# A hybrid decoder layer on one core: the output projection of the state-space heads two pairs at a time, v split for four heads at once, three pairs of split weight tiles

## The chip, the core and the metric

The kernel runs on one core of a Trainium2 chip. A core has a matmul engine (TensorE, PE in the profile, with its weight loads as PEld), VectorE (DVE), ScalarE (ACT), GpSimd (POOL) and SyncE (SP), which here only issues transfers. Each engine works through its own list of instructions in order; they wait for one another by semaphores. The metric is the device time of one execution in microseconds (us); lower is better.

## The reference

One decoder layer on 512 tokens of width 1024, in float32:

```python
h = rms_norm(x, norm_mix_w)
z, xbc, dt_raw, q, k, v, f_raw = jnp.split(h @ w_in, [...], axis=-1)
y_ssd = ssd_mixer(xbc, z, dt_raw, ...)      # 16 heads of 64, 2 groups, chunks of 128 tokens
y_fox = fox_mixer(q, k, v, f_raw, ...)      # 16 heads of 64, causal, with a forget gate
mixed = jnp.concatenate([y_ssd, y_fox], axis=-1)          # 512 x 2048
x = x + mixed @ w_out                                     # 2048 x 1024
hf = rms_norm(x, norm_ffn_w)
x = x + conv_gated_mlp(hf, w_up, ..., w_down)             # 1024 -> 2 x 2816 -> 1024
```

In the attention mixer, q and k are normalised per head, the cumulative sum of log forget gates is added to the logits (`cum[q] - cum[k]`), and `p @ v` follows a softmax. In the state-space mixer (SSD), each chunk of 128 tokens has a product within the chunk and one with the state that the chunks before it left; its output is gated by `silu(z)` and normalised per group.

## The kernel before

**Numbers in two parts.** Every matrix product is made of three matmuls of a reduced float32 type: a high part times a high part, high times low, low times high (`mm3`, lines L110, L111 and L112). Weights come from memory as tiles `wraw` of 128x1024 (512 KB, five buffers, a transfer on SP's queue, L101). `load_split` makes the high part `wh` on ACT (L104) and the low part `wl = wraw - wh` on DVE or POOL (L105); which of the two is a letter of the table `LOW_PART` ("d" is DVE, "p" POOL, and "p" where a key isn't in it), taken in turn. `wh` and `wl` have two buffers each in the pool `wp`; in the last stage, the down projection, `split_unit` adds a third of each from another pool (`pb`).

**Stages.** (1) To about 25 us: x comes in, is split in two, and the norm's scale is computed. (2) To about 225 us the SSD mixer in two groups of 8 heads. `ssd_proj` makes x, B and C (`feature_tile`, then a convolution over tokens on DVE, L351) and the gate (`token_block` into banks named pq, then `gz`, L374 to L376). `dt_f` makes the step sizes; its cumulative sum `cs` (L304, DVE) is read by a small matmul `pt` (L306). `ssd_scan` goes over four chunks; each ends with the normalised `y` (L441, DVE), a PE transpose `yT` (L446), and the parts `msh` and `msl` (L448, ACT, and L449, DVE), which the output projection multiplies. (3) To about 465 us the attention mixer, 16 heads. For each group of four heads `qk_proj` and `v_proj` project; `fox_qk` transposes a pair's k and q (`qkT`, L496), splits them, and copies the two parts of k to the other 64 partitions by two transfers (`ks`, L506); `fox_probs` makes the logits (`S`, L539 and L540) and the softmax; `fox_values` multiplies with v (`o`). A pair of heads gives 128 columns of `mixed`. Between heads, "fillers" with work that doesn't depend on that head are written. (4) The output projection `out_proj` is spread through (2) and (3): it takes one pair of 128-row slabs of `w_out`, and for each half of the 1024 columns and each of four blocks of 128 tokens it runs 6 matmuls of 512 columns into a bank `po` and adds it to `x2`, the residual (L254, DVE). SSD has pairs 0 to 3, attention 4 to 7. (5) The up projection with its convolution and gate, 494 to 743 us. (6) The down projection, in which half of the transfers of `w_down` tiles `T` are issued by POOL and add to what the tile holds (L809).

**PSUM.** `bank` gives one of three banks of 128x512 that the projections share (names g, pq, po, up, X); `mbank` one of four for the mixers' smaller products; `o` has one. 

**Order.** The program writes each engine's work in a certain sequence, but a scheduler then sets the order of the instructions, by a simulated timeline and by priorities (`urgent` puts scans and heads first). So an edit in one place moves instructions of every engine elsewhere. The number of names (as in `yT_990`) only tells one buffer's use from another's.

Of the kernel before, what the change touches and what calls it, by code (L numbers as in the profile page):

```python
# [9 lines left out]
F32R = mybir.dt.float32r  # L10
AF = mybir.ActivationFunctionType
ALU = mybir.AluOpType
# [3 lines left out]
P = 128  # L16
# [3 lines left out]
NTB = SEQ // P  # L20
# [8 lines left out]
HD = 64  # L29
# [5 lines left out]
ACT_SQ = (1, 3, 5, 7)  # L35
LOW_PART = {
    "feat": "pddddddddp",
    "o0": "dp",
    "o2": "dp",
    "o4": "pd",  # L40
    "o5": "pd",
    "o7": "pd",
    "qk1": "dppd",
    "qk2": "pppd",
# [11 lines left out]
def tile_hybrid_layer(  # L56
# [19 lines left out]
    nc = tc.nc  # L76
# [11 lines left out]
    def raw(ap):  # L88
        return ap.bitcast(F32)
# [9 lines left out]
    def load_split(src, sub=None):  # L99
        r = wp.tile([P, 1024], F32, tag="wraw", name="wraw", bufs=5)  # L100
        nc.sync.dma_start(r, src)  # L101
        h = wp.tile([P, 1024], F32R, tag="wh", name="wh")
        l = wp.tile([P, 1024], F32R, tag="wl", name="wl")
        act.copy(h, r)  # L104
        (sub or dve).tensor_tensor(out=l, in0=r, in1=raw(h), op=ALU.subtract)  # L105
        return h, l

    def mm3(o, ah, al, bh, bl, start, stop, grouped=True):
        kw = {} if grouped else {"skip_group_check": True}
        pe.matmul(o, ah, bh, start=start, stop=False, **kw)  # L110
        pe.matmul(o, ah, bl, start=False, stop=False, **kw)  # L111
        pe.matmul(o, al, bh, start=False, stop=stop, **kw)  # L112

    def bank(name="g"):
        return pg.tile([P, 512], F32, tag="g", name=name)
# [42 lines left out]

    px_ctx = ExitStack()
    px = px_ctx.enter_context(tc.tile_pool(name="px", bufs=1))  # L160
    first = [wp.tile([P, 1024], F32R, tag=t, name=t) for t in ("wh", "wl")]
    wdt = px.tile([P, NK, 64], F32R, tag="wdt", name="wdt")

    def load_x(k):
# [45 lines left out]
    for k in range(NK):  # L210
        pe.matmul(pdt[:64, :], wdt[:, k, :], xh[:, k, :], start=k == 0, stop=False, skip_group_check=True)
        pe.matmul(pdt[:32, :], wdt[:, k, 0:32], xl[:, k, :], start=False, stop=k == NK - 1, skip_group_check=True)
        c = slice(k * P, (k + 1) * P)
# [28 lines left out]
    def out_proj(pairs, m, halves=(0, 1)):  # L242
        for half in halves:
            ws = [load_split(wout[pair, half], sub=low_part("o%d" % pairs[0])) for pair in pairs]
            for tb in range(NTB):
                s = slice(tb * P, (tb + 1) * P)
                o = bank("po")
                for n, (h, l) in enumerate(ws):
                    for j in range(2):
                        k = 2 * n + j  # L250
                        c = slice(j * 512, (j + 1) * 512)
                        mm3(o, m[k][0][:, s], m[k][1][:, s], h[:, c], l[:, c], k == 0, k == 2 * len(pairs) - 1)
                dst = x2[:, tb, half * 512 : (half + 1) * 512]
                dve.tensor_add(dst, o, dst)  # L254

    pss_ctx = ExitStack()
    pss = pss_ctx.enter_context(tc.tile_pool(name="pss", bufs=1, reuse_waits="tile"))
# [212 lines left out]

    def v_proj(gi):
        tiles = token_block(wqkv[gi, 2], "v%d" % gi)
        v = [pa.tile([P, NTB, 2, 2 * HD], F32R, tag="v", name="v", bufs=4) for _ in range(2)]
        for pr in range(2):
            for tb in range(NTB):
                c = (tb % 2) * 256 + pr * P
                o = tiles[tb // 2][:, c : c + P].rearrange("p (h d) -> p h d", d=HD)
                act.activation(v[pr][:, tb, :, 0:HD], o, AF.Copy, scale=r[:, tb : tb + 1])
                dve.scalar_tensor_tensor(
                    out=v[pr][:, tb, :, HD:], in0=o, scalar=r[:, tb : tb + 1], in1=raw(v[pr][:, tb, :, 0:HD]),  # L480
                    op0=ALU.mult, op1=ALU.subtract,
                )
        return v

    LO, HI = slice(0, HD), slice(HD, P)
# [64 lines left out]
        return prob  # L550

    def fox_values(head, prob, v, osum):
        lh = head % 2
        own, other = HALVES[head % 2]
        where = {}
        for n, kbs in enumerate(((0,), (1, 3), (2,))):
# [45 lines left out]
    for tb in range(NTB):  # L602
        nc.sync.dma_start(x2[:, tb, :], x[tb * P : (tb + 1) * P, :])
    st1 = ssd_proj(1)
    for pair in range(2):
        out_proj((pair,), m0[2 * pair : 2 * pair + 2])
    with urgent():
        m1 = ssd_scan(1, *st1)
    qk, vs = {}, {}
# [22 lines left out]

    def end_head(n):
        with urgent():
            m = fox_values(n, probs.pop(n), vs[n // 4][n % 4 // 2], pairs[n // 2][2])
        if m is not None:
            mf.append(m)

    fillers = {0: ["q1"], 3: ["v1"], 4: ["q2", "v2"], 5: ["o0"], 8: ["q3"], 9: ["a", "o1"], 10: ["v3"], 12: ["o2"], 15: ["b"]}

    def fill(name):
        if name == "a":
            out_proj((2,), m1[0:2])
        elif name == "b":
            out_proj((3,), m1[2:4])
        elif name[0] == "q":
            project(int(name[1:]))
        elif name[0] == "v":
            project_v(int(name[1:]))
        else:  # L650
            g = int(name[1:])
            out_proj((4 + g,), mf[2 * g : 2 * g + 2])
# [62 lines left out]
        nc.sync.dma_start(rw[:, 0 : (UNITS[u][1] - UNITS[u][0]) * 512], part(q, u))  # L715
        return rw

    turn = [0]

    def split_unit(u, src):  # L720
        n = (UNITS[u][1] - UNITS[u][0]) * 512
        where = pb if turn[0] % 3 == 2 else wp
        turn[0] += 1
        h = where.tile([P, 1024], F32R, tag="wh", name="wh")
        l = where.tile([P, 1024], F32R, tag="wl", name="wl")
        act.copy(h[:, :n], src[:, :n])  # L726
        dve.tensor_tensor(out=l[:, :n], in0=src[:, :n], in1=raw(h[:, :n]), op=ALU.subtract)  # L727
        return h, l
# [225 lines left out]
```

## Time and profile before

| | |
|---|---|
| median of 3 runs | 847.28 us (845.74 to 851.2) |
| the profiled execution | 845.59 us |
| its span, first to last instruction | 843.8 us |
| mean granted TensorE clock | 0.998 |
| instructions | 12403, of these 4590 matmuls |

The profile is one execution, with the start and end of every instruction and what ended the idle time ahead of it. A row of a group has the line of the kernel, the engine, the operation, the tile it writes and those it reads, the shape and the count, then the group's busy time in us and the mean of one instruction in ns, and the idle time of the engine ahead of them with its releaser. The granted clock is the share of TensorE's full clock that the throttle let through.

### The profile page before, as it was taken

How to read it: one execution, taken by the hardware profiler on the slowest of the kernel's cores; microseconds unless marked ns; L12 is line 12 of the kernel's file. 1: busy time of each engine (PE TensorE's matmuls, PEld its weight loads, DVE VectorE, ACT ScalarE, POOL GpSimd, SP SyncE). 2: the span in 40 equal slices, each digit the busy share in tenths (PEclk: the TensorE clock that was granted, in tenths of full speed). 3: DMA queues.
4: the chain of work that ended last, by engine and by line, in shares of the span. 5: the costliest groups of instructions: out<-in, count | busy, mean ns of one | idle time of the engine just before them, and what ended most of it. 6: DMA issues, size and time to landing. Idle time of an engine off the chain costs nothing.

```text
span 843.8 us, 12403 instructions
## 1 busy us (share of the span) xinstructions
PE 810.0 (96%) x4590; PEld 696.6 (83%) x4590; DVE 630.9 (75%) x999; ACT 434.6 (52%) x830; POOL 291.4 (35%) x281
## 2 busy tenths in 40 slices
PE   6999989899989999999999999999999999998987
PEld 4888879779989898798898888888888888875766
DVE  7696998775779788997988767666666667875644
ACT  5456546443567675684575364444444444654432
POOL 3125253375445445135133413333333331332210
PEclk9999999999999999999999999999999999999999
DMA  8424322431442332333331222322222333599972
GB/s 313 164 76 130 100 101 76 133 105 50 140 123 86 104 101 92 96 112 107 95 101 51 95 81 100 99 99 89 91 97 100 100 100 109 160 304 240 241 169 88
DMA packets 32285, 101.63 MB, mean 120 GB/s; under 512 B 4129, under 2 KB 4961, under 8 KB 32225
## 3 DMA queue, kind: packets, MB, share of 16 engines
q1 hardware_dynamic: 28768, 89.31, 32.3%
q0 software_dynamic: 3456, 11.54, 7.0%
q8 instruction: 36, 0.59, 0.3%
q14 instruction: 25, 0.20, 0.1%
HBM read 94.44 MB, written 2.20 MB: 115 GB/s over the span
## 4 chain that ended last, share of the span: by engine, by line
PE 67%; DVE 13%; issue 7%; DMA 6%; POOL 3%; ACT 3%; SPq 0%; DVEq 0%; POOLq 0%; ACTq 0%
PE up L112 9%; PE up L110 9%; PE up L111 9%; DMA T<-in_wdown_dram 4%; PE pq L111 4%; PE pq L112 4%; PE pq L110 4%; PE po L112 3%; PE po L111 3%; PE po L110 3%; DVE xs L351 2%; PE o L580 1%; PE pT L566 1%; POOL ms L122 1%; PE Y L111 1%
## 5 line engine op out<-in xcount | busy, mean ns | idle before, releaser
L104 ACT CAST wh<-wraw 128x1024 fp32r<-128x1024 f32 x103 | 108.4, 1053 | 135.5 <-PE up L111 72.1
L110 PE MATMUL pq<-wh,xh 128*128 128x256 f32 x512 | 146.3, 288 | 0.0
L112 PE MATMUL pq<-wh,xl 128*128 128x256 f32 x512 | 146.2, 286 | 0.0
L111 PE MATMUL pq<-wl,xh 128*128 128x256 f32 x512 | 145.3, 284 | 0.6 <-DVE wl L105 0.6
L112 PE MATMUL up<-hh,wl 128*128 128x512 f32 (+1 forms) x368 | 140.2, 381 | 0.2 <-DVE wl L105 0.2
L111 PE MATMUL up<-hl,wh 128*128 128x512 f32 (+1 forms) x368 | 139.9, 380 | 0.0
L110 PE MATMUL up<-hh,wh 128*128 128x512 f32 (+1 forms) x368 | 139.8, 380 | 0.0
L105 POOL TENSOR_TENSOR wl<-wraw,wh 128x1024 fp32r<-128x1024 f32 x31 | 75.3, 2427 | 107.7 <-ACT wh L104 98.6
L105 DVE TENSOR_TENSOR wl<-wraw,wh 128x1024 fp32r<-128x1024 f32 x72 | 90.3, 1254 | 20.0 <-ACT wh L104 19.9
L111 PEld LDWEIGHTS pq<-wl,xh 128*128 128x128 f32 x512 | 97.8, 191 | 2.1 <-DVE wl L105 1.1
L110 PEld LDWEIGHTS pq<-wh,xh 128*128 128x128 f32 x512 | 97.5, 191 | 1.9 <-issue 1.2
L112 PEld LDWEIGHTS pq<-wh,xl 128*128 128x128 f32 x512 | 97.8, 191 | 0.7 <-issue 0.5
L112 PEld LDWEIGHTS up<-hh,wl 128*128 128x128 f32 x368 | 69.2, 188 | 13.8 <-DVE wl L105 0.4
L111 PEld LDWEIGHTS up<-hl,wh 128*128 128x128 f32 x368 | 69.2, 188 | 13.1
L110 PEld LDWEIGHTS up<-hh,wh 128*128 128x128 f32 x368 | 69.1, 188 | 13.1 <-issue 0.2
L765 DVE TENSOR_TENSOR up<-up,R 128x512 f32<-128x512 f32 x44 | 30.3, 691 | 57.0 <-PE up L112 57.0
L770 DVE SCALAR_TENSOR_TENSOR ua<-up,pc,ua 128x511 f32<-128x511 f32 (+1 forms) x88 | 67.1, 765 | 3.2 <-ACT ua L768 1.7
L526 POOL TENSOR_SCALAR bias<-cum,tokS 128x256 f32<-128x256 f32 (+1 forms) x32 | 22.4, 711 | 88.9 <-DVE nm L541 88.9
L254 DVE TENSOR_TENSOR x<-po,x 128x512 f32<-128x512 f32 x64 | 43.2, 683 | 10.1 <-PE po L112 9.5
L545 ACT ACTIVATE prob<-prob,nm 128x128 f32<-128x128 f32 (+1 forms) x64 | 35.9, 562 | 27.2 <-DVE nm L541 26.9
L780 POOL TENSOR_TENSOR ua<-ua 128x512 f32<-128x512 f32 x11 | 15.0, 1364 | 93.0 <-DVE ua L770 93.0
L727 DVE TENSOR_TENSOR wl<-T,wh 128x1024 fp32r<-128x1024 f32 (+1 forms) x24 | 26.9, 1134 | 26.2 <-ACT wh L726 26.2
(249 smaller groups left out, 1876.9 us busy)
## 6 DMA issues: line engine op xcount, KB each, us to landing
wraw<-in_wup_dram SPq DMA_DIRECT2D x44, 512.0 KB, 3.3
wraw<-in_wqkv_dram SPq DMA_DIRECT2D x24, 512.0 KB, 3.3
T<-in_wdown_dram POOLq DMA_DIRECT2D x20, 512.0 KB, 11.9
wraw<-in_wout_dram SPq DMA_DIRECT2D x16, 512.0 KB, 3.4
wraw<-in_wdown_dram SPq DMA_DIRECT2D x15, 512.0 KB, 4.6
wraw<-in_wxbc_dram SPq DMA_DIRECT2D x11, 512.0 KB, 4.0
T<-in_wdown_dram SPq DMA_DIRECT2D x10, 512.0 KB, 8.0
wraw<-in_wz_dram SPq DMA_DIRECT2D x8, 512.0 KB, 3.4
```

What stands on the lines that cost most here:

```text
L104: act.copy(h, r)
L105: (sub or dve).tensor_tensor(out=l, in0=r, in1=raw(h), op=ALU.subtract)
L110: pe.matmul(o, ah, bh, start=start, stop=False, **kw)
L111: pe.matmul(o, ah, bl, start=False, stop=False, **kw)
L112: pe.matmul(o, al, bh, start=False, stop=stop, **kw)
L254: dve.tensor_add(dst, o, dst)
L351: dve.scalar_tensor_tensor(out=dst[:, s:], in0=xp[:, : SEQ - s], scalar=half_w[:, cw + 3 - s : cw + 4 - s], in1=dst[:, s:], op0=ALU.mult, ...
L526: (dve if qb == 2 else pool).tensor_scalar(out=b, in0=cum[:, :n], scalar1=-1.0, scalar2=edge, op0=ALU.mult, op1=ALU.add)
L545: act.activation(p, p, AF.Exp, scale=-1.0, bias=nm[:, qb : qb + 1], accum_out=sm[:, qb : qb + 1])
L727: dve.tensor_tensor(out=l[:, :n], in0=src[:, :n], in1=raw(h[:, :n]), op=ALU.subtract)
L765: dve.tensor_mul(xp, o, R2)
L770: dve.scalar_tensor_tensor(out=a[:, s:], in0=xp[:, : SEQ - s], scalar=pc[:, cw + 2 - s : cw + 3 - s], in1=a[:, s:], op0=ALU.mult, op1=ALU.add,
```

## The change

1. `out_proj` for the SSD pairs takes two pairs in one accumulation: 12 matmuls go into a bank before it is added to `x2`. Blocks of tokens go in twos, so that two banks are open at once. Pairs 0 and 1 come together behind `ssd_proj(1)`, as before; pairs 2 and 3 come together, the left half of the columns as a filler at head 9 and the right half at head 15, where pair 2 and pair 3 stood. The attention pairs still go one at a time, with two blocks of tokens per step.
2. `v_proj` evacuates all four heads of a block of tokens by one ACT and one DVE instruction of 256 columns, where there were two of 128 on each.
3. `wh` and `wl` have three buffers in one pool throughout.
4. In `LOW_PART`, `o0` and `o2` go from "dp" to "d", and a key `o6` ("pd") is new.
5. The buffer for the descriptors of POOL's transfers is 1024 instead of 2048 bytes.

```diff
 LOW_PART = {
...
-    "o0": "dp",
-    "o2": "dp",
+    "o0": "d",
+    "o2": "d",
     "o4": "pd",
     "o5": "pd",
+    "o6": "pd",
     "o7": "pd",
...
-        h = wp.tile([P, 1024], F32R, tag="wh", name="wh")
-        l = wp.tile([P, 1024], F32R, tag="wl", name="wl")
+        h = wp.tile([P, 1024], F32R, tag="wh", name="wh", bufs=3)
+        l = wp.tile([P, 1024], F32R, tag="wl", name="wl", bufs=3)
...
     def out_proj(pairs, m, halves=(0, 1)):
         for half in halves:
             ws = [load_split(wout[pair, half], sub=low_part("o%d" % pairs[0])) for pair in pairs]
-            for tb in range(NTB):
-                s = slice(tb * P, (tb + 1) * P)
-                o = bank("po")
+            banks = {}
+            for t0 in (0, 2):
                 for n, (h, l) in enumerate(ws):
-                    for j in range(2):
-                        k = 2 * n + j
-                        c = slice(j * 512, (j + 1) * 512)
-                        mm3(o, m[k][0][:, s], m[k][1][:, s], h[:, c], l[:, c], k == 0, k == 2 * len(pairs) - 1)
-                dst = x2[:, tb, half * 512 : (half + 1) * 512]
-                dve.tensor_add(dst, o, dst)
+                    for tb in (t0, t0 + 1):
+                        s = slice(tb * P, (tb + 1) * P)
+                        if n == 0:
+                            banks[tb] = bank("po")
+                        for j in range(2):
+                            k = 2 * n + j
+                            c = slice(j * 512, (j + 1) * 512)
+                            mm3(
+                                banks[tb], m[k][0][:, s], m[k][1][:, s], h[:, c], l[:, c],
+                                k == 0, k == 2 * len(pairs) - 1,
+                            )
+                        if n == len(ws) - 1:
+                            dst = x2[:, tb, half * 512 : (half + 1) * 512]
+                            dve.tensor_add(dst, banks[tb], dst)
...
-        v = [pa.tile([P, NTB, 2, 2 * HD], F32R, tag="v", name="v", bufs=4) for _ in range(2)]
-        for pr in range(2):
-            for tb in range(NTB):
-                c = (tb % 2) * 256 + pr * P
-                o = tiles[tb // 2][:, c : c + P].rearrange("p (h d) -> p h d", d=HD)
-                act.activation(v[pr][:, tb, :, 0:HD], o, AF.Copy, scale=r[:, tb : tb + 1])
-                dve.scalar_tensor_tensor(
-                    out=v[pr][:, tb, :, HD:], in0=o, scalar=r[:, tb : tb + 1], in1=raw(v[pr][:, tb, :, 0:HD]),
-                    op0=ALU.mult, op1=ALU.subtract,
-                )
+        v = pa.tile([P, NTB, 4, 2 * HD], F32R, tag="v", name="v", bufs=2)
+        for tb in range(NTB):
+            c = (tb % 2) * 256
+            o = tiles[tb // 2][:, c : c + 256].rearrange("p (h d) -> p h d", d=HD)
+            act.activation(v[:, tb, :, 0:HD], o, AF.Copy, scale=r[:, tb : tb + 1])
+            dve.scalar_tensor_tensor(
+                out=v[:, tb, :, HD:], in0=o, scalar=r[:, tb : tb + 1], in1=raw(v[:, tb, :, 0:HD]),
+                op0=ALU.mult, op1=ALU.subtract,
+            )
...
-    for pair in range(2):
-        out_proj((pair,), m0[2 * pair : 2 * pair + 2])
+    out_proj((0, 1), m0)
...
-    fillers = {0: ["q1"], 3: ["v1"], 4: ["q2", "v2"], 5: ["o0"], 8: ["q3"], 9: ["a", "o1"], 10: ["v3"], 12: ["o2"], 15: ["b"]}
+    fillers = {
+        0: ["q1"], 3: ["v1"], 4: ["q2", "v2"], 5: ["o0"], 8: ["q3"], 9: ["a0", "o1"], 10: ["v3"], 12: ["o2"],
+        15: ["a1"],
+    }
...
-        if name == "a":
-            out_proj((2,), m1[0:2])
-        elif name == "b":
-            out_proj((3,), m1[2:4])
+        if name[0] == "a":
+            out_proj((2, 3), m1, halves=(int(name[1:]),))
...
-    turn = [0]
-
     def split_unit(u, src):
         n = (UNITS[u][1] - UNITS[u][0]) * 512
-        where = pb if turn[0] % 3 == 2 else wp
-        turn[0] += 1
-        h = where.tile([P, 1024], F32R, tag="wh", name="wh")
-        l = where.tile([P, 1024], F32R, tag="wl", name="wl")
+        h = wp.tile([P, 1024], F32R, tag="wh", name="wh", bufs=3)
+        l = wp.tile([P, 1024], F32R, tag="wl", name="wl", bufs=3)
...
-    nc = _bacc.Bacc("TRN2", target_bir_lowering=False, num_devices=1, dynamic_dma_scratch_size=2048)
+    nc = _bacc.Bacc("TRN2", target_bir_lowering=False, num_devices=1, dynamic_dma_scratch_size=1024)
```

The scheduler moves instructions with it. In the changed kernel the line numbers are a few higher (L101 becomes L102, L506 L513, L446 L454, the matmuls L111 to L113). Three places:

SP's queue where the first attention pair begins; `wraw` are the q, k and v weights, `cum` the forget gate's sums, `ks` the copies of k for the two heads of a pair. Before:

```order
L101 DMA wraw<-in_wqkv_dram 128x1024 x5
L512 DMA cum<-cf_d 128x512 x2
L101 DMA wraw<-in_wqkv_dram 128x1024
L512 DMA cum<-cf_d 128x512 x2
L101 DMA wraw<-in_wqkv_dram 128x1024
L506 DMA ks<-ks 64x1024 x2
L101 DMA wraw<-in_wqkv_dram 128x1024
```

and with the change:

```order
L102 DMA wraw<-in_wqkv_dram 128x1024 x5
L519 DMA cum<-cf_d 128x512 x2
L102 DMA wraw<-in_wqkv_dram 128x1024
L519 DMA cum<-cf_d 128x512 x2
L513 DMA ks<-ks 64x1024
L102 DMA wraw<-in_wqkv_dram 128x1024
L513 DMA ks<-ks 64x1024
```

The `wraw` that stood ahead of both `ks` now stands between them.

PE at the third transpose of the first scan (`yT_990`; `pq` is the gate's projection, `cb` the next chunk's product). Before:

```order
L110 MATMUL pq_1467<-wh_1471,xh_93 128x256
L111 MATMUL pq_1467<-wl_1472,xh_93 128x256
L112 MATMUL pq_1467<-wh_1471,xl_94 128x256
L446 MATMUL yT_990<-ident_75,y_969 128x128 x4
L411 MATMUL cb_1012<-cT_377,bT_376 128x128
```

and with the change:

```order
L111 MATMUL pq_1341<-wh_1399,xh_93 128x256
L112 MATMUL pq_1341<-wl_1400,xh_93 128x256
L113 MATMUL pq_1341<-wh_1399,xl_94 128x256
L454 MATMUL yT_990<-ident_75,y_969 128x128 x4
L419 MATMUL cb_1012<-cT_377,bT_376 128x128
```

The transpose now stands in the projection with weights `wh_1399`, the one ahead of that with `wh_1471`. Counted from the program's start, the matmuls of 256 and of 512 columns ahead of `pt` and of the first scan's transposes are:

| ahead of | before, 256 and 512 | with the change |
|---|---|---|
| `pt` | 97, 145 | 63, 145 |
| first `yT` | 192, 219 | 192, 187 |
| second | 194, 292 | 192, 266 |
| third | 303, 294 | 255, 294 |
| fourth (`yT_1039`) | 384, 307 | 370, 295 |

On DVE, ahead of `cs` there are three convolution steps fewer; ahead of the first `y` three convolution steps and two products `xp` fewer; of the second, three steps, one `xp` and one `xs` product; of the third, one `gz` and one `xs` product; of the fourth none.

PE at the first output projection. Before, where `po_1615` is the third block of tokens:

```order
L111 MATMUL po_1607<-wl_1596,msh_822 128x512
L112 MATMUL po_1607<-wh_1595,msl_823 128x512
L446 MATMUL yT_1039<-ident_75,y_1024 128x128 x4
L411 MATMUL cb_1768<-cT_1055,bT_1054 128x128
L110 MATMUL po_1615<-wh_1595,msh_822 128x512
L111 MATMUL po_1615<-wl_1596,msh_822 128x512
```

and with the change, where `po_1605` and `po_1612` are the first two blocks:

```order
L111 MATMUL pq_1468<-wh_1525,xh_93 128x256
L454 MATMUL yT_1039<-ident_75,y_1024 128x128 x4
L419 MATMUL cb_1752<-cT_1055,bT_1054 128x128
...
L112 MATMUL pq_1468<-wl_1526,xh_93 128x256
L113 MATMUL pq_1468<-wh_1525,xl_94 128x256
L111 MATMUL po_1605<-wh_1595,msh_822 128x512
L112 MATMUL po_1605<-wl_1596,msh_822 128x512
L113 MATMUL po_1605<-wh_1595,msl_823 128x512
```

The last transpose of the scan, which stood between two blocks of the output projection, now stands in the gate's projection ahead of it, and both weights' parts of the first two blocks come before the third block.

More of the change, by code (lines that the diff above doesn't have):

```diff
@@ L160, in tile_hybrid_layer @@
     px = px_ctx.enter_context(tc.tile_pool(name="px", bufs=1))
-    first = [wp.tile([P, 1024], F32R, tag=t, name=t) for t in ("wh", "wl")]
+    first = [wp.tile([P, 1024], F32R, tag=t, name=t, bufs=3) for t in ("wh", "wl")]
     wdt = px.tile([P, NK, 64], F32R, tag="wdt", name="wdt")
@@ L552, in fox_values @@
     def fox_values(head, prob, v, osum):
-        lh = head % 2
+        lh = head % 4
         own, other = HALVES[head % 2]
@@ L634, in end_head @@
         with urgent():
-            m = fox_values(n, probs.pop(n), vs[n // 4][n % 4 // 2], pairs[n // 2][2])
+            m = fox_values(n, probs.pop(n), vs[n // 4], pairs[n // 2][2])
         if m is not None:
             mf.append(m)
-    fillers = {0: ["q1"], 3: ["v1"], 4: ["q2", "v2"], 5: ["o0"], 8: ["q3"], 9: ["a", "o1"], 10: ["v3"], 12: ["o2"], 15: ["b"]}
+    fillers = {
+        0: ["q1"], 3: ["v1"], 4: ["q2", "v2"], 5: ["o0"], 8: ["q3"], 9: ["a0", "o1"], 10: ["v3"], 12: ["o2"],
+        15: ["a1"],
+    }
     def fill(name):
-        if name == "a":
-            out_proj((2,), m1[0:2])
-        elif name == "b":
-            out_proj((3,), m1[2:4])
+        if name[0] == "a":
+            out_proj((2, 3), m1, halves=(int(name[1:]),))
         elif name[0] == "q":
```

## The prediction

> **What bounds the kernel now.** I begin with the page's totals, since they say which engine a saving must reach.
>
> ```profile
> span 843.8 us, 12403 instructions
> PE 810.0 (96%) x4590; PEld 696.6 (83%) x4590; DVE 630.9 (75%) x999; ACT 434.6 (52%) x830; POOL 291.4 (35%) x281
> PE 67%; DVE 13%; issue 7%; DMA 6%; POOL 3%; ACT 3%; SPq 0%; DVEq 0%; POOLq 0%; ACTq 0%
> ```
>
> PE is busy 96% of the span, and the third line, the chain that ended last, runs on PE for 67%. The change keeps all 4590 matmuls, so it can gain no more than PE's gaps and its slow stretches. A table of stretches says where those are; its columns are start and end, length, the busy time (and instructions) of PE, weight loads, DVE, ACT and POOL, the granted clock, the DMA share and GB/s.
>
> ```profile
> 40.00:140.00 100.00, 95.03 (x595) 83.58 (x594) 89.08 (x126) 53.55 (x133) 39.62 (x26) 1.00 0.32 106
> 220.00:240.00 20.00, 17.06 (x130) 16.69 (x129) 12.24 (x26) 10.29 (x23) 11.59 (x14) 0.92 0.47 133
> 520.00:540.00 20.00, 20.00 (x90) 16.57 (x89) 13.67 (x18) 9.17 (x13) 6.42 (x6) 1.00 0.31 104
> ```
>
> In the up projection (520 to 540) PE has no gap: 90 matmuls of 512 columns in 20 us are 0.222 us each. I use 0.23 for a matmul of 512 columns. In the mixer there are gaps, and in 220 to 240 the granted clock falls to 0.92 as well. Over the first scan (40 to 140) DVE is nearly full: some 89 of 100 us. What PE waited for there, in us in total, times, and the longest:
>
> ```profile
> PE S L539 <- DMA ks<-ks: 3.4, 2, 2.9
> PE qkT L496 <- DVE tok L468: 2.5, 2, 1.3
> PE yT L446 <- DVE y L441: 1.7, 1, 1.7
> PE pt L306 <- DVE cs L304: 1.5, 1, 1.5
> PE po L110 <- ACT msh L448: 1.5, 1, 1.5
> PE po L110 <- DVE v L479: 1.2, 1, 1.2
> PE po L110 <- ACT th L375: 0.7, 1, 0.7
> PE pq L111 <- DVE wl L105: 0.6, 1, 0.6
> ```
>
> These eight rows, 13.1 us, are what the change can reach in the mixer.
>
> **The change part by part.** First the work on the engines beside PE.
>
> ```profile
> L254 DVE TENSOR_TENSOR x<-po,x 128x512 f32<-128x512 f32 x64 | 43.2, 683 | 10.1 <-PE po L112 9.5
> L105 POOL TENSOR_TENSOR wl<-wraw,wh 128x1024 fp32r<-128x1024 f32 x31 | 75.3, 2427 | 107.7 <-ACT wh L104 98.6
> L105 DVE TENSOR_TENSOR wl<-wraw,wh 128x1024 fp32r<-128x1024 f32 x72 | 90.3, 1254 | 20.0 <-ACT wh L104 19.9
> L478 ACT ACTIVATE v<-pq,r 128x128 fp32r<-128x128 f32 x32 | 11.4, 364 | 19.8 <-DVE v L479 13.1 <-PE pq L112 6.5
> L479 DVE SCALAR_TENSOR_TENSOR v<-pq,r,v 128x128 fp32r<-128x128 f32 x32 | 10.9, 347 | 4.2 <-ACT v L478 3.8
> L460 ACT ACTIVATE tok<-pq,r 128x256 f32<-128x256 f32 x32 | 15.1, 471 | 8.3 <-PE pq L112 8.3
> ```
>
> Adding two pairs in one accumulation removes 16 of the 64 adds: 16 x 0.683 = 10.9 us of DVE. Seven low parts go from POOL to DVE: 7 x 2.427 = 17.0 us off POOL, 7 x 1.254 = 8.8 us onto DVE. The wide v instructions are not in the trace. On ACT one of 256 columns stands in the tok row, 0.471 us: 16 x 0.471 = 7.5 instead of 11.4 us. On DVE I bound the wide one by one and two of the narrow ones, 0.35 and 0.69 us, and take 0.47 again, since a narrow one costs about the same on both engines: 16 x 0.47 = 7.5 us instead of 10.9. Together DVE loses some 5.5 us of 630.9, ACT 4, POOL 17. None of this is on PE, which covers it: I count it at nothing, in itself. If the cover went (DVE last everywhere) it would be worth those 5.5 us.
>
> So the sum is made of waits. **The first ks transfer.**
>
> ```profile
> 228.89 0.38 SPq L101 DMA_DIRECT2D wraw<-in_wqkv_dram  x1
> 230.24 2.41 SPq L506 DMA_DIRECT2D ks<-ks  x2
> 235.51 0.34 SPq L101 DMA_DIRECT2D wraw<-in_wqkv_dram  x1
> 233.12 2.36 POOL L105 TENSOR_TENSOR wl<-wraw,wh 128x1024 fp32r<-128x1024 f32 x1 [2.92 <-ACT wh L104]
> 237.12 0.44 PE L539 MATMUL S<-ks,qs 128*128 128x128 f32 x1 [2.94 <-DMA ks<-ks]
> DMA to landing us min/median/max: 2.8/2.9/6.7
> ```
>
> The ks of head 0 was issued at 230.24, 1.35 us behind a 512 KB wraw, and took the 6.7 us that is the maximum of all 16 (median 2.9). PE stood 2.94 us for it, and behind it the clock fell: a mean of 0.92 over 20 us is 0.08 x 20 = 1.6 us lost, 1.7 with the ends of the stretch. In the new order that wraw stands behind the first ks. With 2.9 to 4 us to land, ks arrives at 233.1 to 234.2, when PE asks (237.12 - 2.94 = 234.2). Bounds: the whole 2.9 + 1.7 goes, or none of it; I take the whole, since what made it late is moved past it. Late next is the ks of head 1: it now stands behind the wraw, and that one waits for a free buffer, as the third row shows (issued 0.03 us after POOL's wl ended at 235.48). The third wl buffer lets that wl run earlier; if it doesn't, this is a rival below.
>
> [...]
>
> **The other waits that go.** po behind th and msh (0.7 + 1.5): the new order ends the z projection first, and puts the last y transpose of the scan ahead of all po; the po that needs its chunk comes 14 matmuls of 256 and 24 of 512 columns later, 14 x 0.12 + 24 x 0.23 = 7.2 us behind it, which is more than the two waits of before together with the work that lay between. Bounds 0 and 2.2, I take 2.2. po behind v (1.2) is a bank that is read late; a v bank is now given back after the second of four instructions, not after the sixth of eight: 1.2. pq behind wl (0.6): with three buffers the low part is computed one tile further ahead: 0.6.
>
> **The first scan.** Here the order moves PE's waiting instructions forward by more than DVE's.
>
> ```profile
> 62.41 2.88 DVE L351 SCALAR_TENSOR_TENSOR xs<-xp,half_w,xs 128x510 f32<-128x510 f32 x1
> 65.40 0.74 DVE L351 SCALAR_TENSOR_TENSOR xs<-xp,half_w,xs 128x509 f32<-128x509 f32 x1
> 66.53 0.38 PE L306 MATMUL pt<-cs,carry 128*128 128x1 f32 x2 [1.47 <-DVE cs L304]
> 94.42 1.46 DVE L441 SCALAR_TENSOR_TENSOR y<-y,ss,nwb 128x512 f32<-128x512 f32 x1
> 98.41 0.60 PE L446 MATMUL yT<-ident,y 128*128 128x128 f32 x4
> 120.30 2.86 DVE L441 SCALAR_TENSOR_TENSOR y<-y,ss,nwb 128x512 f32<-128x512 f32 x1 [0.80 <-POOL ss L122]
> 123.21 0.66 PE L446 MATMUL yT<-ident,y 128*128 128x128 f32 x4 [1.72 <-DVE y L441]
> 141.10 0.74 DVE L441 SCALAR_TENSOR_TENSOR y<-y,ss,nwb 128x512 f32<-128x512 f32 x1
> 141.94 0.60 PE L446 MATMUL yT<-ident,y 128*128 128x128 f32 x4
> 156.60 0.75 DVE L441 SCALAR_TENSOR_TENSOR y<-y,ss,nwb 128x512 f32<-128x512 f32 x1 [0.67 <-POOL ss L122]
> 158.76 0.60 PE L446 MATMUL yT<-ident,y 128*128 128x128 f32 x4
> ```
>
> From the order, ahead of each: pt has 34 matmuls of 256 columns less ahead of it, at 0.12 us (0.23 by halves) 4.1 us; DVE's cs has three convolution steps less, 3 x 0.74 = 2.2. If DVE is the limit, pt waits 1.9 longer. The first y transpose comes 32 matmuls of 512 columns earlier (7.3, less the 1.9 lost: 5.4); DVE has three convolution steps and two xp products less ahead of its y, 3.6; 2.5 us of slack (95.88 to 98.41) cover it. The second: 26 matmuls of 512 columns, 5.9 - 1.9 = 4.0, against 3.6, so 0.4 more. The third: 48 matmuls of 256 columns, 5.8 - 2.3 = 3.5 against one gz and one xs product, 1.2, with a slack of 0.1 (141.84 to 141.94): 2.3 more. At the fourth PE is level again, and 1.4 us of slack cover the rest. In all 1.9 + 0.4 + 2.3 = 4.6 us lost if DVE is never idle; nothing if all that DVE waits for also comes sooner. DVE idles 10.9 of these 100 us, so I take 3.0, nearer the upper end.
>
> Two of these waits have a DVE instruction of 2.9 us ahead of them that elsewhere takes 0.74. [...]
>
> Last, at the end of the mixer one po finds its bank only two matmuls after the old content ended, 0.5 us against an add of 0.68: +0.4 with the rest of the queue.
>
> **Sum**, against the profiled execution (845.59 us, 1.8 more than its span): -2.9 - 1.7 - 2.2 - 1.2 - 0.6 + 3.0 + 0.4 = -5.2, so 840.4 us. The median of the runs, 847.28, lies 1.7 above that execution: **842.1 us**. With the scan at its two ends, 839 to 844.
>
> **The rivals.**
>
> *The ks wait moves to head 1.* For: the wraw between the two ks, which waits for POOL. Against: the third buffer. Then 2.9 + 1.7 stay: 846.7.
>
> *PE follows the new order without new waits, and all eight rows go.* For: 24 to 32 matmuls more between producer and consumer at most places, three buffers. Against: a DVE that is nearly full between 40 and 140. -13.1 - 1.7 = -14.8: 832.5.
>
> *DVE holds the scan to the full, and the clock falls there.* pt would wait 1.47 + 1.9 = 3.4 us, longer than the 2.94 that halved the clock. +4.6 + 1.7 for my +3.0: 845.4.
>
> *Only the work behind PE is saved*, and no wait changes in sum: 847.3.
>
> *The smaller ring slows the tail: slower.* Half the buffer for the transfers that POOL issues could hold fewer of them at a time.
>
> ```profile
> L809 POOL DMA_DIRECT2D T<-in_wdown_dram x24: 848/853/1132, 739.6 to 812.3; - x24
> DMA to landing us min/median/max: 4.4/10.5/19.9
> 760.00:780.00 20.00, 16.92 (x67) 11.70 (x67) 11.19 (x12) 9.44 (x10) 5.12 (x6) 1.00 1.07 240
> ```
>
> 24 of them are issued in 72.7 us, 3.0 apart, and take 10.5 (median of all T transfers), so 3.5 are under way on average. If only three fitted, they would take 72.7 x 3.5 / 3 = 84.8 us, 12 more, and the end with them: 854. It decides from fewer than four at a time on. Against: the DMA share there is 1.07, so that fewer at a time would each land sooner.
>
> **How the numbers follow.** Forecast 0.38, ks to head 1 0.18, all waits gone 0.20, DVE with the clock 0.10, no change in waits 0.08, ring 0.06. A measurement of this kernel tells about 1% from no change, 8.5 us: faster is below 838.8, slower above 855.8. Faster: most of "all waits gone" and the low end of the forecast, 0.17 + 0.08 = 0.25. Slower: a third of the ring and a little for ks and clock together in the worst case, 0.05. The rest is 0.70. The range must reach into the 832.5 and past 847.3 with the scan's spread of 1.6: 833.5 to 850.
>
> **What will show it.** PE's wait for ks under 1 us in all and the clock 1.00 where S begins; no po row with msh, th or v; pt at 2.5 to 3.5 us and the third y transpose with a wait; 48 adds, 79 and 24 low parts; up projection at 0.222 us a matmul. I am wrong if a ks of head 1 is the wait, if DVE's cs and y come early enough, if new waits at heads 2 to 15 appear that the order doesn't tell, or if the T transfers are issued later than now.

## The result, and the profile after

The changed kernel takes 843.99 us (median of 9 runs, 840.16 to 845.99), the kernel before 847.70 us in its 9 runs beside it (845.74 to 851.98). The ratio is 0.9943, with a 95% interval of 0.9924 to 0.9962: 4.8 us less, where 5.2 us were forecast. The profiled executions, 843.69 and 845.59 us, lie closer together than that, because the one of before had a mean granted clock of 0.998, while 74 runs of that kernel have 0.994 on average; the changed kernel's has 0.991.

The page after has the same totals, in the same order as before: span, busy time of each engine, and the engines' shares of the chain that ended last.

```profile
span 841.9 us, 12399 instructions
PE 812.6 (97%) x4590; PEld 700.0 (83%) x4590; DVE 619.9 (74%) x974; ACT 431.9 (51%) x814; POOL 280.0 (33%) x274
PE 75%; DVE 12%; DMA 7%; issue 3%; ACT 2%; POOL 1%; SPq 0%; DVEq 0%; ACTq 0%; POOLq 0%
```

The groups that the change touches:

```profile
L262 DVE TENSOR_TENSOR x<-po,x 128x512 f32<-128x512 f32 x48 | 32.4, 684 | 8.4 <-PE po L113 8.1
L106 DVE TENSOR_TENSOR wl<-wraw,wh 128x1024 fp32r<-128x1024 f32 x79 | 101.7, 1287 | 27.9 <-ACT wh L105 27.8
L106 POOL TENSOR_TENSOR wl<-wraw,wh 128x1024 fp32r<-128x1024 f32 x24 | 60.9, 2540 | 85.8 <-ACT wh L105 81.2 <-DVE xs L364 4.6
L486 DVE SCALAR_TENSOR_TENSOR v<-pq,r,v 128x256 fp32r<-128x256 f32 x16 | 7.6, 481 | 3.8 <-ACT v L485 3.5
L485 ACT ACTIVATE v<-pq,r 128x256 fp32r<-128x256 f32 x16 | 7.6, 472 | 7.6 <-PE pq L113 6.7 <-DVE v L486 0.8
```

48 adds, 79 and 24 low parts, and a wide v of 0.47 and 0.48 us: the work came out as counted. DVE lost 11 us in all, twice what the counts give (5.5 us), since other instructions ran shorter too: the eight `tok`, for one, took 13.9 us in all where they took 19.3. The stretches (busy PE, weight loads, DVE, ACT and POOL, granted clock, DMA share, GB/s):

```profile
0.00:20.00 20.00, 13.81 (x48) 9.27 (x48) 14.42 (x16) 12.58 (x20) 11.73 (x13) 0.91 0.87 315
20.00:40.00 20.00, 18.40 (x76) 14.51 (x77) 12.62 (x24) 6.02 (x9) 1.40 (x2) 0.91 0.52 187
40.00:140.00 100.00, 92.20 (x542) 79.43 (x541) 87.88 (x124) 53.01 (x128) 40.15 (x24) 0.99 0.31 102
120.00:140.00 20.00, 16.03 (x90) 13.68 (x91) 18.34 (x22) 8.25 (x23) 6.37 (x4) 0.94 0.33 107
220.00:240.00 20.00, 20.00 (x170) 20.00 (x169) 13.48 (x23) 12.26 (x24) 12.99 (x16) 1.00 0.40 126
520.00:540.00 20.00, 20.00 (x89) 16.54 (x89) 13.30 (x17) 8.03 (x11) 6.41 (x6) 1.00 0.32 105
800.00:820.00 20.00, 18.17 (x72) 14.20 (x71) 9.48 (x10) 7.01 (x8) 3.44 (x4) 0.91 0.78 166
```

220 to 240, where ks was waited for, is now full, at a clock of 1.00. The up projection is as before. The first scan has more gaps (PE busy 92.2 of 100, 95.0 before), and the clock falls at four new places: twice in the first 40 us, once behind 136 us (0.94 in 120 to 140), once in the tail. What PE waited for:

```profile
PE g L213 <- DVE xl L183: 5.6, 4, 3.9
PE st L436 <- DVE xdt L434: 2.4, 1, 2.4
PE yT L454 <- DVE y L449: 1.9, 1, 1.9
PE S L546 <- DMA ks<-ks: 1.6, 1, 1.6
PE xT L368 <- DVE xs L364: 1.4, 2, 0.9
PE pt L320 <- DVE cs L315: 1.3, 1, 1.3
PE po L111 <- DVE x L262: 0.3, 1, 0.3
PE pt L314 <- DVE cs L312: 0.2, 1, 0.2
```

No po waits for th, msh or v any more, no pq for wl, and no qkT for tok; the 1.6 us of S is at 287 us, at another pair of heads. New are a longer gap at the start (g for xl: 4.3 before with 1.8 as the longest, 5.6 now with one gap of 3.9) and st in the first scan (0.7 before, 2.4 now).

### The profile page after: what moved, and what is told of

It is laid out like the page before. It is cut to its first block, busy times and chain, and to the rows that moved or that the text cites. A ratio compares the mean times of both kernels' runs of the same rounds, so it can differ in the third digit from the quotient of the medians.

```text
span 841.9 us, 12399 instructions
## 1 busy us (share of the span) xinstructions
PE 812.6 (97%) x4590; PEld 700.0 (83%) x4590; DVE 619.9 (74%) x974; ACT 431.9 (51%) x814; POOL 280.0 (33%) x274
## 4 chain that ended last, share of the span: by engine, by line
PE 75%; DVE 12%; DMA 7%; issue 3%; ACT 2%; POOL 1%; SPq 0%; DVEq 0%; ACTq 0%; POOLq 0%
PE up L111 10%; PE up L112 10%; PE up L113 9%; PE pq L113 7%; PE pq L112 7%; PE pq L111 7%; PE po L111 4%; PE po L112 4%; PE po L113 4%; DMA T<-in_wdown_dram 3%; DVE xs L359 3%; PE o L587 2%; PE pT L573 2%; DMA wraw<-in_wdown_dram 2%; PE yd L423 1%
## 5 line engine op out<-in xcount | busy, mean ns | idle before, releaser
L111 PE MATMUL pq<-wh,xh 128*128 128x256 f32 x512 | 148.2, 289 | 0.0
L112 PE MATMUL pq<-wl,xh 128*128 128x256 f32 x512 | 147.9, 289 | 0.0
L113 PE MATMUL pq<-wh,xl 128*128 128x256 f32 x512 | 146.3, 286 | 0.0
L111 PE MATMUL up<-hh,wh 128*128 128x512 f32 (+1 forms) x368 | 140.0, 381 | 0.0
L113 PE MATMUL up<-hh,wl 128*128 128x512 f32 (+1 forms) x368 | 139.7, 380 | 0.0
L106 DVE TENSOR_TENSOR wl<-wraw,wh 128x1024 fp32r<-128x1024 f32 x79 | 101.7, 1287 | 27.9 <-ACT wh L105 27.8
L113 PEld LDWEIGHTS pq<-wh,xl 128*128 128x128 f32 x512 | 98.4, 192 | 1.2 <-issue 0.7
L111 PEld LDWEIGHTS pq<-wh,xh 128*128 128x128 f32 x512 | 98.2, 192 | 1.2 <-issue 0.7
L106 POOL TENSOR_TENSOR wl<-wraw,wh 128x1024 fp32r<-128x1024 f32 x24 | 60.9, 2540 | 85.8 <-ACT wh L105 81.2
L111 PEld LDWEIGHTS up<-hh,wh 128*128 128x128 f32 x368 | 69.1, 188 | 13.3 <-issue 0.2
L113 PEld LDWEIGHTS up<-hh,wl 128*128 128x128 f32 x368 | 69.2, 188 | 13.2
L533 POOL TENSOR_SCALAR bias<-cum,tokS 128x256 f32<-128x256 f32 (+1 forms) x32 | 25.0, 792 | 77.5 <-DVE nm L548 74.4
L729 ACT CAST wh<-T 128x1024 fp32r<-128x1024 f32 (+1 forms) x24 | 23.4, 976 | 38.5 <-DMA T<-in_wdown_dram 32.2
```

Source lines behind the costliest of these rows:

```text
L533: (dve if qb == 2 else pool).tensor_scalar(out=b, in0=cum[:, :n], scalar1=-1.0, scalar2=edge, op0=ALU.mult, op1=ALU.add)
```

## The experiments

Each kernel was timed against the kernel before on the same chip. The first four have one part of the change each. Where two of them reach the same waits, their gains can't add up; that was the second question.

**Part 2 alone, the wide v** (the diff of `v_proj` above, the indices in `fox_values` that go with it, and nothing else):

> The kernel before with part 2 alone (v of four heads at once). My theory, that the gain is made of single waits and that each hangs on the order of a few instructions: the wait of po for v (1.2 us) goes, the wraw stays ahead of both ks, so PE's wait for ks stays near 3 us with a fall of the clock behind it; ratio to before 0.997 to 1.000. Rival, that work saved on DVE and ACT is what counts: 16 instructions less on each give 3 to 7 us, ratio 0.992 to 0.996.

Measured: 839.71 us, ratio 0.9908 (0.9884 to 0.9933), outside both ranges. By the medians this part alone is worth more than the whole change (0.9943; the intervals just overlap), though it saves less work than part 1: 3.2 us on DVE and 3.9 on ACT. All waits of qkT for tok and of po for v are gone from its list, and the wait for ks, which was to stay near 3 us, is 1.4. Between the first qkT and the last o, where the kernel before has five rows of PE's waits with 8.4 us (S 3.4, qkT 2.5, po for v 1.2, pT 0.7, pq 0.6), two are left:

```profile
PE S L538 <- DMA ks<-ks: 1.4, 1, 1.4
PE S L538 <- DVE ks L503: 0.4, 1, 0.4
```

With them went the fall of the clock at 237 us (0.50 in 237 to 240 before, 1.00 there now). The experiments further down ask which part of the edit did it.

**Part 1 alone, two pairs in one accumulation** (with `"o0": "dppp"` and `"o2": "dppp"`):

> The kernel before with part 1 alone (two pairs in one accumulation), and the letters of LOW_PART chosen so that as many low parts stay on DVE and POOL as before. My theory: the waits of po for msh and th (2.2 us together) go, the wait for ks stays near 3 us, since the wraw still stands ahead of both ks; ratio 0.996 to 0.999. Rival, that the 16 adds less (10.9 us of DVE) count by themselves: ratio 0.988 to 0.993.

Measured: 853.47 us, ratio 1.008 (1.0056 to 1.0104): slower, against both expectations, though 48 adds instead of 64 stand in its trace. Its two longest rows of PE's waits:

```profile
PE qkT L503 <- DVE tok L475: 6.4, 3, 3.9
PE po L110 <- ACT wh L104: 4.0, 2, 2.0
```

The second row is new: a bank needs the weights of both pairs, and with two buffers the next half's can't be prepared meanwhile. The first row is explained below.

**Part 4 alone, the low parts on DVE** (the three letters of `LOW_PART`):

> The kernel before with part 4 alone: the low parts of pairs 0 and 2 on DVE, one of pair 6 too (77 instead of 72 on DVE, 26 instead of 31 on POOL, since pairs 1 and 3 keep their own keys here). My theory: nothing that PE waits for is reached, ratio 0.998 to 1.002. Rival, that DVE instructions stretched to 2.3 to 2.9 us beside a POOL low part are what PE's waits come from: five such stretches less, each worth up to 2 us, ratio 0.993 to 0.997.

Measured: 847.95 us, ratio 1.0011 (0.9993 to 1.0029); three low parts moved here, not five (75 on DVE, 28 on POOL). No change, as the theory had it. The waits of qkT for tok are still 2.5 us, so this says nothing against low parts on POOL that do lie beside an instruction that PE waits for.

**Parts 3 and 5 alone, three buffers and the smaller ring:**

> The kernel before with parts 3 and 5 alone (three buffers of split weights, and the smaller ring, without which they find no room). My theory: the waits for wl and qkT between 240 and 350 us (0.6 and 2.5) go, since low parts are computed a tile ahead; but as in the changed kernel the second POOL low part comes at 17 us already, holds up a DVE instruction of 0.2 us by 2, and PE's gap there grows from 2.0 to 4.0 us with a fall of the clock (1.7); the wait for ks stays near 3 us. Ratio 0.997 to 1.001. Rival, that the third buffer carries the whole gain: ratio 0.993 to 0.996, with no such gap.

Measured: 840.90 us, ratio 0.9939 (0.9921 to 0.9957). Half a miss: the gap at the start is there (3.9 us) and the clock falls behind it (0.50 in 21 to 23), but the gain is larger than I gave it, because not only qkT and pq but also po's waits are gone, and S waits 0.9 us instead of 3.4. This one part, with the old v and the old output projection, has the ratio of the whole change (0.9943).

**Wide v and three buffers together**, with the old output projection:

> The kernel before with parts 2, 3 and 5 (wide v, three buffers, the smaller ring), but with the output projection and LOW_PART of before. If v and the buffers reach different waits, their ratios multiply: 0.9908 x 0.9939 = 0.985, some 834 us. Rival, that both reach the same waits (qkT and wl between 240 and 350 us, the clock behind ks): 0.989 to 0.992, no better than v alone. My theory is in between, since the third buffer brings the gap of 4 us and the fall of the clock at 17 to 24 us along: 0.986 to 0.989.

Measured: 842.03 us, ratio 0.9945 (0.9924 to 0.9967). The rival is right that the two don't add up, but the ratio lies above all three ranges: together they look slower than v alone (0.9884 to 0.9933; the intervals just overlap). Parts 1 and 4, which separate this kernel from the whole change (0.9943), are worth nothing on top. That both reach the same waits can be read from the profiled executions. The stretch is from PE's first qkT to the end of its last o, about 230 to 460 us; the kernels with three buffers have a few more matmuls in it.

| kernel | length, us | PE idle in it, us | falls of the clock in it |
|---|---|---|---|
| before | 232.9 | 8.4 | 1 |
| wide v alone | 223.6 | 1.9 | 0 |
| three buffers alone | 224.3 | 0.9 | 0 |
| wide v and three buffers | 226.7 | 1.7 | 1 |
| the change | 228.0 | 1.6 | 0 |

Either part alone takes nearly all of the 8.4 us, and it can go only once.

**Two pairs in one accumulation with three buffers:**

> The kernel before with parts 1, 3 and 5: two pairs in one accumulation, with three buffers; as many low parts on DVE and POOL as before. Alone, part 1 was slower by 0.8%, with 4.0 us of po waiting for wh. Theory 1, that two pairs at a time need the third buffer, since both pairs' weights must be there before a bank can be finished: the waits of po for wh go, and the ratio is that of the buffers or a little better, 0.991 to 0.996. Rival, that the longer filler itself holds up the heads (qkT waited 3.9 us for tok at 395 us): that wait stays, ratio 0.998 to 1.003.

Measured: 842.77 us, ratio 0.9939 (0.9918 to 0.9961), the same as the buffers without it (0.9939). The waits of po for wh are gone. So part 1 costs 0.8% with two buffers and nothing with three, and it gains nothing with either, although DVE has 16 adds less: those lie beside PE's work.

**Where does v's gain come from?** Two kernels separate the release of its banks from the wide instructions. First the 32 narrow ones in another order:

```diff
-        for pr in range(2):
-            for tb in range(NTB):
+        for tb in range(NTB):
+            for pr in range(2):
```

> The kernel before, with its 32 narrow v instructions on each of ACT and DVE, but in the order of the blocks of tokens, so that the first bank is read out after four of eight and not after six. Theory 1, that wide v gains by giving its banks back early: the wait of po for v (1.2 us) goes and at least half of the gain stays, ratio 0.992 to 0.996. Theory 2, that it gains by the 16 instructions less on each engine, which let tok start ahead of the POOL low part beside it: ratio 0.998 to 1.001, and the two waits of qkT for tok (2.5 us) stay, with a tok of 3.4 us ahead of each.

Measured: 846.97 us, ratio 1.0002 (0.9984 to 1.0020). Then the wide ones, with the bank given back one instruction later:

```diff
-        for tb in range(NTB):
+        for tb in (0, 2, 1, 3):
```

> The kernel before with wide v, but its blocks of tokens read out in the order 0, 2, 1, 3, so that the first bank is given back after the third of four instructions and not after the second. Theory 1 (banks): a wait of po or pq for v comes back, some 0.5 to 1.2 us at one or two places, ratio 0.992 to 0.996. Theory 2 (fewer instructions): as wide v, 0.989 to 0.993, and no wait of qkT for tok.

Measured: 839.09 us, ratio 0.9911 (0.9891 to 0.9932). So the release of the banks is worth nothing, as the second theory had it; the gain comes with the wide instructions. Their number isn't the only thing that changes with them, though. The scheduler leaves PE's matmuls in the order of before up to the first S and sets hundreds behind it in another place, in both kernels with the wide v alike; with the narrow v read out in another order all but some 80 of the 4590 stay. No kernel has 16 instructions less in the old order, so the lower number and the new order aren't separated. The waits of the first of the two kernels are still those of before:

```profile
PE qkT L496 <- DVE tok L468: 2.5, 2, 1.3
PE po L110 <- DVE v L479: 1.2, 1, 1.2
```

The 7.8 us are mostly the waits that went (8.4 to 1.9 us) and the fall of the clock. How a wait of PE can go when work on other engines is saved or moved is seen at one of the instructions that PE waits for. In the kernel before, `tok` and the POOL low part beside it (start and length in us):

```profile
332.90 2.40 POOL L105 TENSOR_TENSOR wl<-wraw,wh 128x1024 fp32r<-128x1024 f32 x1
332.96 3.41 DVE L468 TENSOR_TENSOR tok<-tok,ms 128x1024 f32<-128x1024 f32 x1 [1.85 <-POOL ms L122]
```

and with the wide v:

```profile
324.97 1.23 DVE L468 TENSOR_TENSOR tok<-tok,ms 128x1024 f32<-128x1024 f32 x1
325.09 3.34 POOL L105 TENSOR_TENSOR wl<-wraw,wh 128x1024 fp32r<-128x1024 f32 x1
```

Whichever of the two begins first, by 0.06 or 0.12 us, runs at its own length, and the other ends about its own length behind it: with POOL ahead, POOL takes 2.40 us and tok 3.41, ending 1.07 behind POOL; with tok ahead, tok takes 1.23 and POOL 3.34, ending 2.23 behind tok. PE waits for tok, never for that low part. Two of the three tok of 3.40 to 3.42 us in the kernel before became short with the wide v (at 273 and 325 us), and PE's 2.5 us went with them. All 112 tok of the 14 profiles agree: 1.2 to 1.4 us without a low part on POOL beside it or with one that began later; with one that began 0.06 to 0.08 us ahead 3.35 to 3.43, 0.44 us ahead 3.02, 0.57 us ahead 2.91, 1.2 us ahead 2.3. In part 1 alone it went the other way: a POOL low part began 0.07 us ahead of a tok at 395.57 us, which then took 3.35 us, and PE waited 3.9.

**One low part taken off POOL, in the kernel before** (`"qk2": "dppd"` for `"pppd"`):

> The kernel before with one low part moved from POOL to DVE, the one that POOL begins at 278.82 us, 0.06 us ahead of a tok of 3.42 us (others take 1.22). The matmuls stay in the same order. If a POOL low part holds the tok instruction up: tok takes 1.2 us, PE's wait there (1.3 us at 281) goes although DVE now has 1.25 us more to do, and the execution is 1 to 2 us shorter behind it: ratio 0.997 to 0.999. If the wait is DVE's own load: it stays or grows, 1.000 to 1.003.

The instruction came out as expected, with one row of the profile to show it:

```profile
282.97 1.23 DVE L468 TENSOR_TENSOR tok<-tok,ms 128x1024 f32<-128x1024 f32 x1 [2.80 <-POOL ms L122]
```

1.23 instead of 3.42 us, and one of the two waits of qkT is gone (1.3 left of 2.5). The time is 845.62 us, ratio 0.9992 (0.9975 to 1.0010): it can't be told from no change, and the 1 to 2 us are neither shown nor excluded. In its profiled execution, ks took 8.3 us and PE waited 4.5 us for it.

**The same step in the kernel with the wide v, at the first scan** (`"z1": "ddpd"` for `"pdpd"`):

> The kernel with wide v alone, with one more low part moved to DVE: the one beside which DVE's y took 2.86 us, ahead of PE's wait of 1.7 us at the second transpose of the first scan (121.8 us). By the theory that POOL holds DVE up: y takes 0.74 us, the wait falls to 0.5 to 1, and the kernel is 1 to 2 us faster than with wide v alone, ratio 0.988 to 0.991 against before. Rival: DVE is nearly full there (19.3 of 20 us), so 1.25 us more of it make the waits no smaller: 0.990 to 0.993.

Measured: 836.80 us (834.15 to 838.39), ratio 0.9880 (0.9862 to 0.9899), the fastest of all, and clearly faster than the changed kernel. Against wide v alone (0.9908, and 0.9911 for the kernel with the later release) it is 0.003 less, but the intervals overlap, so that the step's own gain is likely and not certain. In place of 2.86 us:

```profile
119.67 0.75 DVE L441 SCALAR_TENSOR_TENSOR y<-y,ss,nwb 128x512 f32<-128x512 f32 x1 [0.80 <-POOL ss L122]
```

and PE's wait of 1.7 us for y is gone from its list. That DVE is nearly full there did no harm: 1.25 us more work took away a hold of 2.1.

**Two low parts taken off POOL in the changed kernel** (`"feat": "dddddddddp"`, `"z1": "pddd"`), one at the start, one at the wait of st. The places, in the changed kernel:

```profile
14.90 5.46 POOL L106 TENSOR_TENSOR wl<-wraw,wh 128x1024 fp32r<-128x1024 f32 x2 [2.02 <-ACT wh L105]
18.14 2.26 DVE L221 TENSOR_SCALAR half_w<-pc 128x68 f32<-128x68 f32 x1
21.12 0.42 PE L213 MATMUL g<-xl,wdt 128*32 128x512 f32 x1 [3.89 <-DVE xl L183]
133.31 2.34 POOL L106 TENSOR_TENSOR wl<-wraw,wh 128x1024 fp32r<-128x1024 f32 x1 [9.43 <-ACT wh L105]
133.53 2.67 DVE L434 TENSOR_TENSOR xdt<-xdt,dte 128x512 f32<-128x512 f32 x1
136.35 1.10 PE L436 MATMUL st<-xdt,b_tok 128*128 128x512 f32 x2 [2.38 <-DVE xdt L434]
```

The third buffer lets POOL begin its second low part at once (both are done at 20.36 us; before, the second began at 21.57), and DVE's `half_w`, 0.18 us before, takes 2.26 us; the xl behind it begins at 20.33 us, 17.81 before, and PE is late with it.

> The changed kernel, with two more low parts moved from POOL to DVE: the second at the start (17.4 us), and the one at 133.3 us, beside which DVE's xdt took 2.67 instead of 0.68 us. Theory, that PE's gaps in front of a fall of the clock come from DVE instructions that POOL's low part holds up: the gap at 17 us falls from 4 to 2 us, the wait of st from 2.4 to under 1, and the falls of the clock at 21 and 137 us go, each worth 1.7 us; in all 4 to 7 us, ratio 0.986 to 0.990 against 0.994 of the changed kernel. Rival, that the gaps are DVE's own load, which now grows by 2.5 us: 0.993 to 0.997.

Measured: 842.78 us, ratio 0.9951 (0.9930 to 0.9972), no better than the changed kernel. The hold at the start is gone, and no wait of st stands in its list; two rows of its timeline, and the two rows of its waits that grew:

```profile
18.98 0.18 DVE L221 TENSOR_SCALAR half_w<-pc 128x68 f32<-128x68 f32 x1
18.44 0.63 PE L213 MATMUL g<-xl,wdt 128*32 128x512 f32 x1 [1.45 <-DVE xl L183]
```

```profile
PE xT L368 <- DVE xs L364: 3.7, 3, 1.5
PE g L111 <- DVE xp L352: 1.9, 1, 1.9
```

PE's gap at the start is 1.45 instead of 3.89 us, but xT waits for xs 3.7 instead of 1.4 us and g for xp 1.9 more, so the rival holds here: with these two more low parts DVE is late a few us behind. The next kernel, with the start's low part alone moved, has the same two rows (3.6 and 1.9). And the clock still fell at 8 and 18 us, and once more at 39, behind the wait for xp. The start differs from kernel to kernel without this step too: wide v with three buffers and two pairs with three buffers, whose second low part is on POOL as in the changed kernel, have 2.3 and 1.4 us as their longest gap there; that `half_w` came after that low part and another instruction was held is my reading, and no row here shows it.

**The wide v, three buffers, and the start's second low part on DVE:**

> As the kernel with wide v, three buffers and the old output projection, but with the second low part of the start on DVE. By the same theory its gap at 17 us is 2 us and not 4, and the clock doesn't fall at 21 us: ratio 0.002 to 0.0045 below that kernel's. Rival: the same as that kernel, within 0.002.

Measured: 841.83 us, ratio 0.9932 (0.9906 to 0.9957), against 0.9945 (0.9924 to 0.9967) without that edit. The difference, 0.0013, is inside both intervals: inconclusive.

## Why the prediction was right, step by step

The time came out 0.4 us from the forecast's difference. Two terms of the sum stood where they were put; one had its size but not its place; and two that I left out have opposite signs and nearly cancel, so that 0.4 us is in part luck. By stages of the two profiled executions: up to the first qkT the changed kernel is 5.4 us longer (1.5 us of idle more and three falls of the clock), from there to the end of the mixer 9.0 shorter (6.4 us of idle and one fall less), behind that 1.6 longer (one fall, 0.5 us of idle).

**ks (-2.9 and -1.7): right.** The rows of SP's queue after the change, and then the time from issue to landing of all 16 ks:

```profile
235.67 0.53 SPq L513 DMA_DIRECT2D ks<-ks  x1
236.30 1.60 SPq L102 DMA_DIRECT2D wraw<-in_wqkv_dram  x1
237.99 0.47 SPq L513 DMA_DIRECT2D ks<-ks  x1
```

```profile
DMA to landing us min/median/max: 2.8/2.9/6.1
```

The first ks landed 3.55 us after its issue, and PE didn't wait; that of head 1, behind the wraw, took 5.09, and PE didn't wait for it either. All profiles of this study agree with the cause that was given, though no kernel moves the wraw alone: with the wraw 1.35 to 1.5 us ahead of the first ks (eight kernels) it took 5.99 to 8.31 us; with the wraw 0.4 us ahead (two) 4.75 and 5.01; with the wraw behind it (four, the changed kernel among them) 3.55 to 4.18. What I didn't see is that PE needn't wait as long for it: the wide v alone leaves the wraw ahead, and S waits 1.4 us with no fall of the clock: there are 57 matmuls between the first qkT and the first S instead of 50, and ks landed in 6.1 us instead of 6.7.

**po and pq (-2.2, -1.2, -0.6): right in size.** All four rows are gone, and the last term, +0.4 at the end of the mixer, is the po that waits 0.3 us for x. The reasons are less sure than the sizes. Three buffers alone, with the old output projection and the old v, have none of the four rows, so part 1's own order isn't needed for the 2.2; and pq's wait for wl is gone with the wide v alone too. The release of v's bank, which I gave as the reason for the 1.2, is not it: with the early release and narrow v the wait stays at 1.2, with the late release and wide v it is gone.

**The first scan (+3.0 between 0 and 4.6): the size was right, the places wrong.** pt lost nothing in all (1.5 before, 0.2 and 1.3 now, the second a later matmul that waits for cs), and the third transpose doesn't wait. Instead xT grew from 0.8 to 2.0, yT from 1.7 to 1.9 and st from 0.7 to 2.4: 3.1 us. The order told that DVE would be the limit in that stretch; it couldn't tell which of DVE's instructions a POOL low part would hold up. A fall of the clock behind st (0.94 from 120 to 140 us) comes on top.

**Left out: qkT for tok, 2.5 us gained.** I took the saved work on DVE and ACT at nothing, because PE covers it. That step failed: an edit beside PE also shifts when instructions begin, and in the rows of tok that decides which of the two engines holds up the other (3.41 us with the POOL low part 0.06 us ahead, 1.23 with tok 0.12 us ahead). I had named two long instructions of the scan only (2.88 and 2.86 us against 0.74), and never asked where else a POOL low part lies beside an instruction that PE waits for. For the changed kernel the third buffer is the nearest reason, since with it alone no wait of qkT for tok is left. Two tok of the changed kernel still were held up, one of 2.91 us at 391.20 and the one below, and PE waited for neither, so a hold need not cost anything:

```profile
275.75 2.40 POOL L106 TENSOR_TENSOR wl<-wraw,wh 128x1024 fp32r<-128x1024 f32 x1
275.82 3.42 DVE L476 TENSOR_TENSOR tok<-tok,ms 128x1024 f32<-128x1024 f32 x1
```

**Left out: the start and the clock, lost.** The gap at 17 us grew from 1.8 to 3.9 us, behind the low part that the third buffer lets begin earlier. The share of full clock that is missing, times the time, is an upper estimate of what is lost to it, since a slow stretch can lie beside idle time; averaged over the runs:

| kernel | runs | mean granted clock | us lost at most |
|---|---|---|---|
| before | 74 | 0.9941 | 5.0 |
| wide v alone | 6 | 0.9947 | 4.5 |
| three buffers alone | 12 | 0.9908 | 7.7 |
| wide v and three buffers | 12 | 0.9896 | 8.8 |
| the change | 9 | 0.9920 | 6.7 |

That is up to 1.7 us more for the change, and up to 3 for three buffers alone. Within the runs of one kernel the time grows by 0.56 us for each us of this product (195 runs of 14 kernels), so about 1 and 1.5 us are nearer. It accounts for wide v and buffers together looking slower than v alone, but not for their not adding up: less the loss the two would be at 833.6 us together and 835.0 and 833.7 apart (medians of time less loss), with 0.56 of it at 837.2, 837.2 and 836.6. Either way the three are level, as they would be if both parts reach the same waits. I had put the loss of the clock into one rival, at pt, and not into the sum.

**The rivals.** The ks wait didn't move to head 1. "All eight rows go" came half true: six of the eight are gone or halved (S, qkT, three of po, pq), but the first scan, the start and the clock took some of it back. The smaller ring cost nothing that can be told apart: POOL issues each transfer as fast as before (a median of 856 ns, 853 before), the 24 of them over 75.4 us instead of 72.7, and the T transfers land sooner (median of all 9.0 instead of 10.5 us). The forecast's arithmetic for this rival mixed two queues: the 10.5 us hold SP's T transfers as well, and POOL's alone took 12.4, so 4.1 of them were under way and not 3.5 (9.6 us with the change).

```profile
L812 POOL DMA_DIRECT2D T<-in_wdown_dram x24: 848/856/1052, 735.7 to 811.1; - x24
DMA to landing us min/median/max: 5.4/9.0/13.6
```

It was not tried alone.

## What to carry to other kernels

Run the parts of a change one by one: here wide v gave 0.9% alone, the buffers 0.6% alone, two pairs in one accumulation were slower by 0.8% without the buffers, and the bundle gave 0.6%. Two parts that reach the same waits of the bottleneck don't add up (0.9908 and 0.9939 alone, 0.9945 together). Beside a POOL low part some DVE instructions here took about three to twelve times their usual time (tok 3.42 us against 1.23, y 2.86 against 0.75, `half_w` 2.26 against 0.18); look for such an instruction ahead of a PE wait, and for the POOL instruction that began just before it; moving that one POOL instruction is a cheap thing to try. Of four such moves here one seems to have gained (0.3% on top of the wide v, 2.1 us of PE's idle gone from the SSD mixer in its profile) and three can't be told from no change, because other waits grew; the 16 adds less gained nothing. A deeper buffer let an engine start earlier here, and so hold up something that had been in front of it: POOL's second low part, which began at 21.57 us before, now lies beside `half_w` at 18.14.

## What the runs showed of the hardware

The granted clock fell behind gaps shorter than the 2.94 us ahead of 237.12 in the kernel before: in the changed kernel behind the 2.38 us before st (136.35; a mean of 0.94 over 120 to 140), and behind two gaps of 1.30 and 0.53 us near each other (804.40 and 805.66; 0.91 in 800 to 820). In single microseconds it was 0.50 at the bottom, from 237 to 240 in the kernel before, from 138 to 141 and from 807 to 810 in the changed one. Other gaps of that size brought no fall (2.06 us at 749 in the changed kernel with two more low parts moved), and the runs of one kernel differ by it: 842.4 us at a clock of 0.999 and 851.6 at 0.985 are two runs of the kernel before. A DVE instruction of 0.18 us stood 2.26 us beside a POOL low part, so it isn't long DVE instructions alone that were held up here.
